# Soft mixture-of-experts on one core: 92 subtractions and additions go from VectorE to GpSimd, and two more pairs of products are split

## The chip, the cores and the metric

One Trainium2 chip, one of its cores. The metric is the device time of one execution in microseconds (us); the figure of a kernel is the median of its runs.

## The reference

Every token is multiplied with the weights of all eight experts, and the results are added with the softmax of the router's logits as weights. There are 16 x 512 = 8192 tokens of 512 features, 8 experts, and 2048 output columns:

```python
probs = softmax(router_logits)                 # 8192 x 8
output = np.zeros((batch, seq, expert_hidden))
for e in range(n_experts):
    output += probs[:, :, e:e+1] * np.matmul(x, expert_weights[e])
```

Seen as one matrix product, the left operand has 8192 rows and 8 x 512 = 4096 inner elements (x scaled by each expert's probability), the right one 4096 x 2048.

## The kernel before

**The products.** The matrix product is done with Winograd's form of Strassen's algorithm: split in two along rows, inner dimension and columns, it takes seven products of halves instead of eight, at the price of additions. The kernel does this twice. On the outer level the rows are 16 groups `q` of 512 tokens, each a block `2q` and a block `2q+1` of 256; the inner halves are experts 0 to 3 and 4 to 7; the column halves are 1024 wide. The seven outer products of a group are called P1 to P7 (`r` in the code); each has 256 tokens, 2048 inner elements and 1024 columns. On the inner level each of them is again seven *steps* (`STEPS`: 1, 5, 6, 2, 7, 3, 4). A step is eight matmuls of 128 rows, 128 inner elements and 512 columns, in float16, summed in one PSUM bank of float32. The tiles of a result are named by `tn`, the half of the tokens and the half of the columns.

**Stages.** The products are done outer product by outer product, in *stages* that mostly hold two of them (a pair), interleaved step by step: P1, then P2, then P5 and P6 mixed (a stage holds P6 of group q and P5 of group q+1; the first P6 stage and the last one hold a single product, P6 of group 0 and of group 15), then P7 and P4 in turn for the same pair of groups, then P3. A pair's stage has 14 *slots*, one for each step of each product. `k5`, `k6`, `k7` and `k3` are the numbers of the first P5 stage, the last P6 stage, the first P7 stage and the first P3 stage.

**Who does what.** TensorE does the matmuls. VectorE (`tt`, L113) makes the left operands (x times probability, minus what was there), the differences of weights, and the additions that combine a result with a base. ScalarE copies PSUM banks. GpSimd (`pool`, L127) issues stores, casts on loading and accumulating stores; it computes nothing but one mask at the start. SyncE issues the remaining loads. Each engine works through its instructions in the program's order.

**What sets the order.** The order is written out when the program is built. `at(stage, slot, f)` hangs a function on a slot. VectorE's work that is not bound to a bank is put into a queue with `later(cost, make)`: `slack` keeps one clock for TensorE and one for VectorE and takes tasks out of the queue while VectorE's clock, advanced by each task's cost, lies behind TensorE's; `need(task)` empties the queue as far as a task that is wanted now. What is not queued is issued where its function is called.

**P6's bases.** The four result tiles of P6 in group q are added on to a *base*: a kept tile of P1 (`kept`, fetched by SyncE into a tile `h`) minus P5's tile of the same name. `joined(q, tn)` (L1171) queues this subtraction with cost 0.69 in front of VectorE's queue, at slots 12, 13 and 13 of the stage before and at slot 3 of P6's own stage, for the tiles (0,0), (1,1), (0,1) and (1,0); where the stage before holds one product alone, at its slots 5, 6 and 6. `post_on_base` (L743) reads the bases when steps 1, 5, 6 and 4 are done. After step 1 it writes the sum into a new bank, and step 6 goes on in the bank that it has just read.

**The split of step 1 in P7.** In some P7 stages (`by_ones`, L1044) step 1 of the pair's two products is done as a third level: with the two products as the row halves, four inner chunks each and column halves of 256, it is seven small products of four matmuls of 256 columns. `Ones` (L622) makes what they need of the left operands: the four tiles `s[5]`, `s[6]`, `s[3]`, `s[7]` of 128 x 512 float16, one operation each (the second reads the first, the third the second), queued right behind the first halves of the two left operands, during the P4 stage before. `ones_sum` makes the four sums of the weights once, at slots 9 and 10 of the stages `ONES - 4` and `ONES - 2`; they stay until P7 and P4 are done. `ONES = k7 + 6` is the first such stage, and every second stage after it is one up to `k3`: five of the eight P7 stages.

Of the kernel before, what the change touches and what calls it, by code (L numbers as in the profile page):

```python
# [31 lines left out]
def kernel(  # L32
# [7 lines left out]
    nc = tc.nc  # L40
# [3 lines left out]
    ADD, SUB, MUL = mybir.AluOpType.add, mybir.AluOpType.subtract, mybir.AluOpType.mult  # L44
# [29 lines left out]
    def x_tile():  # L74
        return xpool.tile([P, C, HQ], f16, name="xs", tag="x")
# [7 lines left out]
    def half():  # L83
        return h_tile([P, NB], f32)
# [16 lines left out]
    def note(i):  # L101
        last[i.ins.engine] = i.ins
        if ordered[0]:
            tc.keep_in_program_order(i)

    def dve(i):
        last[i.ins.engine] = i.ins
        tc.keep_in_program_order(i)
# [3 lines left out]
    def tt(o, a, b, op):  # L112
        dve(nc.vector.tensor_tensor(out=o, in0=a, in1=b, op=op))  # L113
# [12 lines left out]
    def pool(o, i, **how):  # L126
        note(nc.gpsimd.dma_start(out=o, in_=i, **how))  # L127
# [203 lines left out]
    for n in range(2):  # L331
# [23 lines left out]
        for j in range(4):  # L355
            o = half()
# [22 lines left out]
    def flush(task):  # L379
        while task is not None and not task.done:  # L380
            queue.popleft().run()

    def need(task):
        if task is not None and not task.done:
            flush(task)
            clock["pe"] = max(clock["pe"], clock["dve"])

    def later(cost, make, first=False):
        t = Task(cost, make)
        (queue.appendleft if first else queue.append)(t)  # L390
        return t
# [70 lines left out]
    class Left:  # L462
# [11 lines left out]
        def make(self, k):  # L474
            if self.of is not None:
                need(self.of.task[k])
            if self.onto is not None:
                t = self.t[k] = self.onto.half(k)
                u = new_u()
                times(u, k, self.xb, self.pb)  # L480
                tt(t, u, t, SUB)
                return
            t = self.t[k] = new_z()
            times(t, k, self.xb, self.pb)
            if self.less is not None:
                u = new_u()
                times(u, k, *self.less)
                tt(t, t, u, SUB)
            if self.of is not None:
                tt(t, self.of.t[k], t, SUB)  # L490
            if self.kept is not None:
                tt(t, t, self.kept.half(k), SUB)
# [91 lines left out]
    class Thirds:  # L584
# [17 lines left out]
        def queue(self, whole_first=False):  # L602
            self.a.queue_make(0)
            self.b.queue_make(0)
            if whole_first:
                self.a.queue_make(1)
                self.b.queue_make(1)
            for p in (5, 6, 3, 7):
                self.task[p] = later(0.69, lambda p=p: self.make(p))
            for left in (self.a, self.b):  # L610
                left.queue_s2()
            if not whole_first:
                self.a.queue_make(1)
                self.b.queue_make(1)
# [7 lines left out]
    class Ones:  # L622
# [5 lines left out]
        def make(self, p):  # L628
            e0, e1, rows = ds(0, C), ds(C, C), ds(0, HP)
            a, b = self.a.t[0], self.b.t[0]  # L630
            if p in (5, 3):
                self.place = x_tile().rearrange("p (two c) t -> p two (c t)", two=2)
            x, y, op = {5: (b[:, e0, rows], b[:, e1, rows], ADD), 6: (5, a[:, e0, rows], SUB),
                        3: (a[:, e1, rows], 6, SUB), 7: (a[:, e0, rows], b[:, e0, rows], SUB)}[p]
            self.room[p] = self.place[:, 0 if p in (5, 3) else 1]
            o = self.room[p].rearrange("p (c t) -> p c t", c=C)
            tt(o, *(self.s[v] if isinstance(v, int) else v for v in (x, y)), op)
            self.s[p] = o

        def queue(self):  # L640
            for p in (5, 6, 3, 7):
                self.task[p] = later(0.42, lambda p=p: self.make(p))

        def op(self, r):
            need(self.task[7])
# [121 lines left out]
    def out_rows(q, odd, cols, tn):  # L767
        t, n = tn
        return out_f[ds((2 * q + odd) * HQ + t * HP, HP), ds(cols * NH + n * NB, NB)]

    def to_out(q, odd, cols, **how):
        return lambda tn, o: pool(out_rows(q, odd, cols, tn), o, **how)
# [20 lines left out]
    def at(stage, slot, make):  # L793
        hooks.setdefault((stage, slot), []).append(make)
# [6 lines left out]
    right = {r: Right() for r in (2, 5, 6, 7, 4, 3)}  # L801
    right[1] = Right(w, {p: Task(2.29, sums[p]) for p in (6, 7, 4)})
    lefts, xs, ps_, bases = {}, {}, {}, {}
# [6 lines left out]
    def left_of(r, q, fresh=True):  # L810
        a, b = 2 * q, 2 * q + 1
        if r == 1:
            pt = PBlock(a, P1, xp1[q - 2][1] if q in (2, 3) else None)
            if q in (2, 3):
                xs[a] = XBlock(a, xp1[q - 2][0])
            return Left(xblock(a), pt), [xblock(a), pt]
        if r == 2:
            pt = PBlock(a, P2)
            return Left(xblock(a), pt), [xblock(a), pt]
        if r == 7:  # L820
            pt = PBlock(b, P2)
            if q >= KEPT_Z:
                return Left(xblock(b), pt, kept=lefts[6, q]), [xblock(b), pt]
            return Left(xblock(b), pt, onto=ZHalves(q)), [xblock(b), pt]
        if r == 4:
            return Left(lefts[7, q].xb, lefts[7, q].pb), []
        if r == 5:
            pt = PBlock(b, PQ)
            return Left(xblock(b), pt), [xblock(b), pt]
        if r == 6:  # L830
            pt = PBlock(a, P1)
            return Left(xblock(a), pt, of=lefts[5, q]), [xblock(a), pt]
        if r == 3 and (q, 0) in EARLY:
            sources = {k: operand3[q, k] for k in range(2) if (q, k) in EARLY}
            if len(sources) == 2:
                return LoadedLeft(None, None, None, sources), []
            pa = PBlock(a, P2)
            return LoadedLeft(xblock(a), pa, ZHalf(q, z_places[q]), sources), [xblock(a), pa]
        if r == 3 and q < KEPT_Z:
            pt, kept_z = PBlock(a, P2), ZBlock(q)  # L840
            return Left(xblock(a), pt, kept=kept_z), [xblock(a), pt, kept_z]
        pa, pb = PBlock(a, PQ), PBlock(b, PQ)
        return Left(xblock(a), pa, (xblock(b), pb)), [xblock(a), pa, xblock(b), pb]

    def kept_rows(q):
        return lambda tn: kept[q][tn[1], ds(tn[0] * HP, HP), :]

    def product(r, q, **how):
        left, loads = left_of(r, q)
        lefts[r, q] = left  # L850
        p = None
        if r == 1:
            def sink(tn, o):
                pool(kept_rows(q)(tn), o)
            p = Product(right[1], left, sink)
        elif r == 2:
            if q >= ON_BASE or q in WITH_KEPT:
                bases[2, q] = Base(kept_rows(q))
            p = Product(right[2], left, to_out(q, 0, 0), bases.get((2, q)))
        elif r == 5:  # L860
            bases[6, q] = m1 = Base(kept_rows(q))
            m1.task = {}

            p = Product(right[5], left, to_out(q, 1, 0))
        elif r == 6:
            m1 = bases[6, q]

            def base(tn):
                need(m1.task[tn])
                return m1.t[tn]  # L870
            p = Product(right[6], left, to_out(q, 0, 1), base)
        elif r == 7:
            base = products[6, q].o.__getitem__
            if q < KEPT_Z:
                base = bases[7, q] = Base(lambda tn: out_rows(q, 0, 1, tn))
            p = Product(right[7], left, to_out(q, 1, 1), base)
        elif r == 4:
            p = Product(right[4], left, to_out(q, 1, 0, accum_op=ADD), products[7, q].o.__getitem__)
        else:
            p = Product(right[3], left, to_out(q, 0, 1, accum_op=ADD), **how)  # L880
        p.loads = loads
        products[r, q] = p
        return p

    products = {}
# [268 lines left out]
    k7 = k6 + 1  # L1154
# [14 lines left out]
    at(k6 - 1, 7, lambda: claim(products[5, 15].o, (1, 0)))  # L1169

    def joined(q, tn):  # L1171
        m1 = bases[6, q]
        m1.task[tn] = later(0.69, lambda: tt(m1.t[tn], m1.t[tn], products[5, q].o[tn], SUB), True)

    for q in range(16):
        k = k5 + 1 + q
# [270 lines left out]
    for stage, slot, q, k in ((k3 - 1, 2, 11, 0), (k3 - 1, 5, 11, 1), (k3 - 1, 7, 8, 0), (k3 - 1, 9, 5, 0),  # L1447
                              (k3 - 1, 10, 8, 1), (k3 - 1, 12, 5, 1)):
        left = lefts[3, q]
# [73 lines left out]
    def ones_sum(r):  # L1523
# [7 lines left out]
            x, y = {5: (7, 1), 6: (3, 5), 4: (2, 6), 7: (3, 7)}[r]  # L1531
            tt(ones7[r], ones7[x], ones7[y], SUB)
        later(0.69, make)
    ONES = k7 + 6
    for r, where in zip((5, 6, 4, 7), ((ONES - 4, 9), (ONES - 4, 10), (ONES - 2, 9), (ONES - 2, 10))):
        at(*where, lambda r=r: ones_sum(r))
    for stage in range(ONES, k3, 2):
        ones_[stage] = Ones(*(p.left for p in stages[stage]), ones7)
# [102 lines left out]
```

## Time and profile before

| | |
|---|---|
| median of 3 runs | 1351.62 us (1351.12 to 1351.67) |
| the profiled execution | 1351.78 us, of which its span of instructions is 1350.1 us |
| granted TensorE clock | 1.00 |
| instructions | 19508 |
| VectorE, operations and waits | 1483 operations, 1166.9 us busy |
| DMA | 346.26 MB, mean 256 GB/s |

The span is what the profiler saw from the first to the last instruction of the program; 1.7 us of the execution lie outside it. A row of a group of instructions gives line, engine, operation, output<-inputs by the program's tile names, shapes, count, then busy us and mean ns, then the idle time of the engine ahead of them. L136 is the matmul's helper, L113 VectorE's, L127 GpSimd's DMAs; since helpers have one line for everything, groups are told apart by tiles: `h<-h` is a base of P6, `xs<-z` and its kin are the quarters for the split, `ps` and `pt` are PSUM banks, `z` left operands, `d` their differences of token halves.

### The profile page before, as it was taken

The page shows a single profiled execution, that of the slowest core. Times are in us where ns is not written, and L with a number is a line of the kernel's source. Part 1 is how long each engine was busy: PE and PEld are TensorE (multiplying, and loading weights), DVE is VectorE, ACT ScalarE, POOL GpSimd, SP SyncE. Part 2 cuts the span into 40 slices and gives each one's busy share as a digit, 9 for nine tenths or more (in the row PEclk, how much of TensorE's full clock was granted, in tenths as well). Part 3 has the DMA queues.
Part 4 walks back from the last instruction along what each step waited for, and adds up shares of the span by engine and source line. Part 5 has one row for each costly group of instructions (what it writes and reads, how often), then busy time and mean ns, then how long its engine had stood idle before and what let it go on. Part 6 is the DMA issues. An engine that isn't in the chain of part 4 may idle for free.

```text
span 1350.1 us, 19508 instructions
## 1 busy us (share of the span) xinstructions
PE 1344.0 (100%) x7122; PEld 694.3 (51%) x7122; DVE 1166.9 (86%) x1483; ACT 281.9 (21%) x593; POOL 403.9 (30%) x619
## 2 busy tenths in 40 slices
PE   9999999999999999999999999999999999999998
PEld 4465655565544444444444444554555455556564
DVE  7878898989989889797897889889898989898984
ACT  3342423223211111111111100110111111224331
POOL 3123322333323232323312112424334231232342
PEclk9999999999999999999999999999999999999999
DMA  9999989989899999999998889999999989999997
GB/s 181 242 222 240 239 264 242 291 284 290 247 329 282 323 288 286 295 306 265 318 325 265 295 313 189 243 239 216 244 249 226 219 219 310 308 178 230 262 163 132
DMA packets 185392, 346.26 MB, mean 256 GB/s; under 512 B 52176, under 2 KB 81616, under 8 KB 181200
## 3 DMA queue, kind: packets, MB, share of 16 engines
q0 software_dynamic: 84960, 176.72, 58.0%
q1 hardware_dynamic: 97024, 146.15, 35.4%
q10 hardware_dynamic: 3312, 22.15, 4.6%
q8 instruction: 55, 0.90, 0.3%
q14 instruction: 41, 0.34, 0.1%
HBM read 203.19 MB, written 174.26 MB: 280 GB/s over the span
## 4 chain that ended last, share of the span: by engine, by line
PE 98%; DMA 1%; POOL 0%; issue 0%; ACT 0%; POOLq 0%
PE ps L136 77%; PE pt L136 21%; DMA w<-in_expert_weights_dram 1%; POOL w L127 0%; ACT h L1578 0%; POOL ident L234 0%; POOLq L234 0%; POOLq L1625 0%
## 5 line engine op out<-in xcount | busy, mean ns | idle before, releaser
L136 PE MATMUL ps<-w,z 128*128 128x512 f16 (+1 forms) x3884 | 840.0, 372 | 0.0
L136 PEld LDWEIGHTS <-z 128*128 128x128 f16 x5236 | 512.3, 98 | 538.1 <-issue 1.1
L127 POOL DMA_DIRECT2D out_dram<-h x380 | 251.8, 679 | 723.9 <-ACT h L751 321.9
L113 DVE TENSOR_TENSOR h<-ps,h 128x512 f32<-128x512 f32 x318 | 214.9, 686 | 59.1 <-PE ps L136 58.0
L136 PE MATMUL pt<-w,z 128*128 128x512 f16 (+1 forms) x1304 | 253.2, 338 | 0.7 <-DMA w<-in_expert_weights_dram 0.7
L113 DVE TENSOR_TENSOR z<-xT,pT 128x2048 f16<-128x2048 f16 x188 | 226.8, 1217 | 2.2 <-DMA xT<-xs 2.2
L136 PE MATMUL ps<-w,d 128*128 128x512 f16 x880 | 200.7, 379 | 0.0
L738 ACT COPY h<-ps 128x512 f32<-128x512 f32 x102 | 59.8, 586 | 394.0 <-PE ps L136 394.0
L136 PEld LDWEIGHTS <-d 128*128 128x128 f16 x880 | 86.1, 98 | 96.3
L113 DVE TENSOR_TENSOR z<-z,d 128x2048 f16<-128x2048 f16 x110 | 131.8, 1217 | 0.0
L113 DVE TENSOR_TENSOR w<-w 128x1024 f16<-128x1024 f16 (+2 forms) x106 | 116.1, 1114 | 2.6 <-PE ps L136 1.0
L113 DVE TENSOR_TENSOR d<-z 128x1024 f16<-128x1024 f16 x110 | 74.1, 685 | 1.0
L113 DVE TENSOR_TENSOR h<-pt,h 128x512 f32<-128x512 f32 x75 | 51.3, 687 | 27.0 <-PE pt L136 23.9
L751 ACT COPY h<-ps 128x512 f32<-128x512 f32 x54 | 31.6, 586 | 203.5 <-PE ps L136 203.5
L113 DVE TENSOR_TENSOR ps<-ps,h 128x256 f32<-128x256 f32 (+1 forms) x84 | 50.6, 603 | 21.0 <-PE ps L136 15.1
L734 ACT COPY h<-ps 128x512 f32<-128x512 f32 x89 | 49.9, 599 | 70.1 <-PE ps L136 61.3
L127 POOL DMA_DIRECT2D kept<-h x56 | 30.6, 547 | 86.2 <-DVE h L113 48.7
L113 DVE TENSOR_TENSOR z<-z 128x2048 f16<-128x2048 f16 (+1 forms) x52 | 50.5, 978 | 1.5
L730 ACT COPY ps<-ps 128x512 f32<-128x512 f32 x47 | 26.8, 570 | 107.4 <-PE ps L136 59.5
L113 DVE TENSOR_TENSOR h<-h 128x512 f32<-128x512 f32 (+2 forms) x69 | 45.0, 675 | 0.1
L127 POOL DMA_DIRECT2D out_dram<-kept x40 | 42.0, 1150 | 0.2 <-issue 0.2
L136 PEld LDWEIGHTS <-h 128*128 128x128 f16 x384 | 37.6, 98 | 4.3
(109 smaller groups left out, 691.7 us busy)
## 6 DMA issues: line engine op xcount, KB each, us to landing
out_dram<-h POOLq DMA_DIRECT2D x380, 256.0 KB, 7.5
z<-z SPq DMA_DIRECT2D x56, 512.0 KB, 8.7
pT<-p_dram SPq DMA_DIRECT2D x93, 256.0 KB, 8.1
h<-kept SPq DMA_DIRECT2D x88, 256.0 KB, 7.2
w<-wd ACTq DMA_DIRECT2D x20, 1024.0 KB, 8.6
w<-in_expert_weights_dram POOLq DMA_DIRECT2D x33, 512.0 KB, 12.2
xT<-x SPq DMA_DIRECT2D x63, 256.0 KB, 7.8
h<-out_dram SPq DMA_DIRECT2D x60, 256.0 KB, 8.9
```

The lines of the kernel that those rows point to most:

```text
L113: dve(nc.vector.tensor_tensor(out=o, in0=a, in1=b, op=op))
L127: note(nc.gpsimd.dma_start(out=o, in_=i, **how))
L136: note(nc.tensor.matmul(ps, z, w, start=start, stop=stop, skip_group_check=True))
L730: act(nc.scalar.copy(self.banks["b"], x))
L734: act(nc.scalar.copy(o[tn], q if p == 5 else x))
L738: act(nc.scalar.copy(o[TN[p]], b if p == 2 else x))
L751: act(nc.scalar.copy(o[tn], b))
```

## The change

`joined` no longer queues the subtraction for VectorE: it has GpSimd do it (`nc.gpsimd.tensor_tensor`) at the place where it is called, so that it stands in GpSimd's order among the stores. With the task gone, P6 takes its bases without asking for one. `Ones.make` has GpSimd do its four operations, and enters them in the queue with cost 0, so that VectorE's clock does not advance for them. `ONES` becomes `k7 + 2`: the stages `k7 + 2` and `k7 + 4` are split too, seven of the eight, and the sums of the weights are made four stages earlier, the first two of them in the stage before the last P6 stage.

```diff
@@ class Ones, make and queue
-            tt(o, *(self.s[v] if isinstance(v, int) else v for v in (x, y)), op)
+            x, y = (self.s[v] if isinstance(v, int) else v for v in (x, y))
+            note(nc.gpsimd.tensor_tensor(out=o, in0=x, in1=y, op=op))
             self.s[p] = o
...
             for p in (5, 6, 3, 7):
-                self.task[p] = later(0.42, lambda p=p: self.make(p))
+                self.task[p] = later(0.0, lambda p=p: self.make(p))
@@ product
         elif r == 5:
-            bases[6, q] = m1 = Base(kept_rows(q))
-            m1.task = {}
-
+            bases[6, q] = Base(kept_rows(q))
             p = Product(right[5], left, to_out(q, 1, 0))
         elif r == 6:
-            m1 = bases[6, q]
-
-            def base(tn):
-                need(m1.task[tn])
-                return m1.t[tn]
-            p = Product(right[6], left, to_out(q, 0, 1), base)
+            p = Product(right[6], left, to_out(q, 0, 1), bases[6, q])
@@ joined
     def joined(q, tn):
-        m1 = bases[6, q]
-        m1.task[tn] = later(0.69, lambda: tt(m1.t[tn], m1.t[tn], products[5, q].o[tn], SUB), True)
+        o = bases[6, q].t[tn]
+        note(nc.gpsimd.tensor_tensor(out=o, in0=o, in1=products[5, q].o[tn], op=SUB))
@@ the split of P7
-    ONES = k7 + 6
+    ONES = k7 + 2
```

In the built program VectorE has 80 operations fewer, GpSimd 92 more, ScalarE eight copies more, and TensorE 32 matmuls of 512 columns fewer and 56 of 256 more. Between the stores of each P6 turn GpSimd's order is now: six stores, the subtraction for (0,0), one store, those for (1,1) and (0,1), one store, and later that for (1,0). VectorE's remaining operations are the same ones, in a somewhat different order.

## The prediction

> **What bounds the kernel now.** I read the busy shares, the granted clock and the chain that ended last on the page, then TensorE's waits, then its timeline. The page first:
>
> ```profile
> PE 1344.0 (100%) x7122; PEld 694.3 (51%) x7122; DVE 1166.9 (86%) x1483; ACT 281.9 (21%) x593; POOL 403.9 (30%) x619
> PEclk9999999999999999999999999999999999999999
> PE 98%; DMA 1%; POOL 0%; issue 0%; ACT 0%; POOLq 0%
> ```
>
> TensorE is busy for 1344.0 of the 1350.1 us span, at the full granted clock, and the chain is TensorE for 98%. A busy matmul row alone does not prove that there are no holes, so the view of TensorE's waits comes next; these are all its rows (who waited, for whom, us in total, times, longest):
>
> ```profile
> PE every L95 <- DVE h L92: 1.3, 1, 1.3
> PE pt L136 <- DMA w<-in_expert_weights_dram: 0.7, 2, 0.4
> PE ps L136 <- DVE lg L304: 0.3, 1, 0.3
> ```
>
> 2.3 us of waits in all, on the warm-up, the first weights and the first logits; none is in a part that the change touches. There is thus nothing of a stall to win: the change can gain only the matmul time that it takes out, and it loses whatever stall it makes. What a matmul costs is read from its start to the next start, here in TensorE's timeline where a split P7 stage begins (start, us, ..., count):
>
> ```profile
> 922.45 0.60 PE L136 MATMUL pt<-w,z 128*128 128x256 f16 x4
> 922.89 0.60 PE L136 MATMUL pt<-xs 128*128 128x256 f16 x4
> 923.32 1.89 PE L136 MATMUL ps<-w,z 128*128 128x512 f16 x8
> 925.05 0.60 PE L136 MATMUL pt<-xs 128*128 128x256 f16 x4
> ```
>
> Four matmuls of 256 columns take 922.89 - 922.45 = 0.44 us (0.109 each when both rows are taken: 0.87 for eight), eight of 512 columns 925.05 - 923.32 = 1.73 us (0.216 each).
>
> **The change, part by part.**
>
> *Two more split pairs.* Step 1 of both products of a pair is 16 matmuls of 512 columns, 2 x 1.73 = 3.46 us. Split, it is seven small products of four matmuls of 256 columns, 28 x 0.109 = 3.05 us. That is 0.40 us less for a pair, 0.81 us for the two. TensorE has no other change of work.
>
> *What leaves VectorE.* From the groups of VectorE's instructions, shapes kept apart (count | busy us, mean ns | idle before):
>
> ```profile
> L113 DVE TENSOR_TENSOR z<-xT,pT 128x2048 f16<-128x2048 f16 x188 | 226.8, 1217 | 2.2 <-DMA xT<-xs 2.2
> L113 DVE TENSOR_TENSOR h<-h 128x512 f32<-128x512 f32 x66 | 44.0, 689 | 0.1
> L113 DVE TENSOR_TENSOR xs<-z 128x512 f16<-128x512 f16 x10 | 4.2, 422 | 0.2
> L113 DVE TENSOR_TENSOR ps<-pt,xs 128x256 f32<-128x256 f32 x10 | 4.3, 428 | 1.5 <-PE pt L136 1.5
> ```
>
> 64 of the 66 in the second row are P6's bases (4 for each of 16 products): 64 x 0.689 = 44.1 us, or 2.76 us in each P6 stage. The quarters of the five split pairs are 20 of 0.42 (the third row has ten of them): 8.4 us, 1.7 us before each. The two new pairs add four additions like the last row, 4 x 0.43 = 1.7 us, and eight small ScalarE copies. On the path this sum is zero: VectorE is not what TensorE waits for. It only widens VectorE's room.
>
> *What GpSimd gets.* 64 subtractions of 512 float32 and 7 x 4 = 28 operations on 512 float16, among the stores that it issues, in the program's order. The trace has one single computing row of GpSimd:
>
> ```profile
> L234 POOL TENSOR_SCALAR_AFFINE_SELECT ident<-ident x1: 334/334/334, 2.7 to 2.7; 128x128 f16<-128x128 f16 x1
> ```
>
> 128 elements with one input in 0.334 us. From below, the price of one subtraction is VectorE's 0.69; the row times four, with nothing taken as fixed, is 1.34; and twice that, were the second input read after the first, is 2.67. I take 1.34, the same engine's row. The Trainium skill, GPSIMD Engine Reference, section 3.1, gives 4497 ns for an addition of 2048 float32, a quarter of which would be about 1.12 us, an estimate; by it the sum would be the same. No run so far shows it.
>
> *Does it reach TensorE in P6's pair stages?* Here is the turn of two such stages, VectorE, GpSimd and TensorE from the timeline:
>
> ```profile
> 474.76 0.68 DVE L113 TENSOR_TENSOR h<-h 128x512 f32<-128x512 f32 x1
> 478.76 0.70 DVE L113 TENSOR_TENSOR ps<-ps,h 128x512 f32<-128x512 f32 x1 [0.37 <-PE ps L136]
> 482.89 0.68 DVE L113 TENSOR_TENSOR h<-pt,h 128x512 f32<-128x512 f32 x1
> ...
> 475.35 0.54 POOL L127 DMA_DIRECT2D out_dram<-h  x1 [0.26 <-issue]
> 477.24 0.54 POOL L127 DMA_DIRECT2D out_dram<-h  x1 [1.35 <-DVE h L113]
> ...
> 483.74 3.62 PE L136 MATMUL ps<-w,d 128*128 128x512 f16 x16
> ```
>
> In the changed program, base (0,0) stands behind the store of 475.35, bases (1,1) and (0,1) behind that of 477.24. So (0,0) is made from 475.89 to 477.23, and its reader, the addition at 478.76, is in time (at 2.67: 478.56, still in time). That addition itself ends 4.3 us before step 6 at 483.74 needs the bank. (1,1) and (0,1) are made by 479.12 and 480.46, the first read at 482.89. The one store queued behind them leaves after 480.46. Cost: none; the cover is 1.5 us of GpSimd's lead plus 4.3 us of VectorE's.
>
> *And in the two stages of one product*, the first of P6 and the last? There the steps of the product follow twice as fast. The first two rows are of the first such stage, the others of the last:
>
> ```profile
> 416.38 1.64 POOL L127 DMA_DIRECT2D out_dram<-h  x3 [2.45 <-DVE h L113]
> 418.32 0.70 DVE L113 TENSOR_TENSOR ps<-ps,h 128x512 f32<-128x512 f32 x1 [0.44 <-PE ps L136]
> ...
> 768.84 0.70 DVE L113 TENSOR_TENSOR ps<-ps,h 128x512 f32<-128x512 f32 x1 [0.76 <-PE ps L136]
> 770.58 0.69 DVE L113 TENSOR_TENSOR h<-pt,h 128x512 f32<-128x512 f32 x1
> 772.31 0.69 DVE L113 TENSOR_TENSOR h<-ps,h 128x512 f32<-128x512 f32 x1
> ...
> 765.97 1.14 POOL L127 DMA_DIRECT2D out_dram<-h  x2 [1.19 <-DVE h L113]
> ...
> 770.36 1.89 PE L136 MATMUL ps<-w,d 128*128 128x512 f16 x8
> ```
>
> In the last one GpSimd now does: store to 766.51, (0,0) to 767.85, store to 768.39, (1,1) to 769.73, (0,1) to 771.07. The readers are at 768.84, 770.58 and 772.31, so each is met with about 1 us to spare. If each of the three waits for one VectorE operation of 1.22 us (the mean of the kernel's commonest one), (0,1) comes at 774.7, 2.4 us late, of which VectorE's lead (the 0.8 us between 769.54 and 770.36, and the base subtraction that no longer stands behind it) takes half. From nothing to 1.2 us, then, for each of the two stages; I take 0.25 each, nearer the rows as they stand: 0.5 us.
>
> *The quarters before a split stage* are made as soon as the second left operand is ready, which the first of these rows marks:
>
> ```profile
> 913.39 0.43 DVE L113 TENSOR_TENSOR xs<-z 128x512 f16<-128x512 f16 x1
> ...
> 913.17 0.96 POOL L127 DMA_DIRECT2D out_dram<-h  x1
> ```
>
> They now begin on GpSimd behind the store, at 914.1; the first is there at 915.5, the fourth at 919.5. TensorE reads the first at 922.89 (its row stands above) and the next at 925.05: 7.4 and 5.5 us to spare. The stores queued behind them wait up to 5.4 us; base fetches wait for such stores, but are issued a stage ahead. Cost: none. The earlier places of the split (its weight sums move four stages up, beside the end of P6) put 4 x 0.69 = 2.8 us on VectorE, where 2.76 a stage have just left it: none.
>
> **The sum.** 1351.78 (the profiled execution) - 0.81 + 0.5 = 1351.47. The median of the runs is 0.16 below the profiled execution: 1351.3 us.
>
> **The rivals.** For the first, VectorE's load by stage (engine busy us and counts in windows; the fullest P6 stage, 15 of them together, the P7 and P4 part, the last single-product stage):
>
> ```profile
> 667.60:691.80 24.20, 24.20 (x113) 10.94 (x112) 23.08 (x29) 3.50 (x6) 6.97 (x13) 1.00 1.04 336
> 426.00:788.40 362.40, 362.40 (x1681) 164.31 (x1679) 308.92 (x376) 49.59 (x85) 99.24 (x175) 1.00 0.99 299
> 774.00:1151.60 377.60, 377.60 (x2014) 196.95 (x2013) 341.45 (x453) 47.06 (x109) 116.14 (x158) 1.00 0.98 243
> 764.20:776.30 12.10, 12.10 (x58) 5.49 (x57) 11.31 (x15) 1.17 (x2) 2.70 (x5) 1.00 0.73 231
> ```
>
> *1. VectorE stands still while GpSimd subtracts (slower, from a certain length on).* Should an operation of GpSimd keep VectorE from its own operations on two operands in SBUF for all of its length p, a P6 stage costs VectorE 308.92/15 = 20.6 - 2.76 + 4p of 24.16 us. It overflows when p is above (24.16 - 17.84)/4 = 1.58 us. At 1.34 it is 23.2: still hidden on the mean, and in the fullest stage (23.08) 1.5 us over, inside VectorE's lead of 4 us; the two single-product stages pay their 1.2 us each, and the time is 1351.62 - 0.81 + 2.4 = 1353.2, still within the bound. At 2.0 it is 1.7 us a stage, 15 x 1.7 = 25 us: 1376. At 2.67 it is 4.4 us a stage: 66 us, 1417. For it: the last row shows only 0.8 us of idle VectorE in the last single stage. Against it: operations with one operand in PSUM (ps and pt in the rows above) stand between VectorE's others, and the one row of GpSimd points below 1.58. The Trainium skill, SBUF — State Buffer, section "Who interferes with whom", says just this: a VectorE instruction with two SBUF inputs and a GpSimd instruction that reads SBUF exclude each other for the whole instruction. By that rule this rival is what happens, and only p decides its size; the trace of before cannot show it. Chances: 0.12 for the small form (within the bound), 0.16 for p above 1.58.
>
> *2. No exclusion, but p near 2.67.* Then the chain in the single-product stages is late by itself: in the last one (0,1) would be ready at 775.1 against 772.3, about 1.5 us of stall after VectorE's lead; in the first one (0,0) follows the first of the three stores, at 416.92, is ready at 419.6 for an addition that now starts at 418.32, and (0,1) comes at 425.5, 3.7 us late: about 2.2. The time is 1351.62 - 0.81 + 3.7 = 1354.5, just over the bound. The pair stages stay hidden, as shown. Chance 0.08.
>
> *3. Stores that come late.* Were a tile that waits for GpSimd's store missing for a base fetch, each split pair could lose a microsecond or more: 7 x 1 = 7, 1358. Against: GpSimd is busy 116.14 of 377.60 us there. Chance 0.04.
>
> *4. The split does not come about, or gains more.* The built program has 24 matmuls more (-32 of 512 columns, +56 of 256), so it comes about; with no stall to remove, 0.81 us is the most. Chance 0.02 for anything faster by 0.2%.
>
> **How the numbers follow.** The bound of 0.2%, about what a measurement of this kernel can tell from no change, is 2.7 us. The forecast (everything hidden but 0 to 1.2 us in two stages, 1350.8 to 1353.2) has 0.58; with rival 1's small form, "same" is 0.70. "Slower" is 0.16 + 0.08 + 0.04 = 0.28, "faster" 0.02. The range goes from 1350.5 (no stall at all, 0.3 for the spread of runs) up through rival 2 and most of rival 3 to 1357.0; rival 1's large form is left out.
>
> **What would show it.** Right: 56 more matmuls of 256 columns and TensorE's list of waits still near 2.3 us, without rows at L136 in P6 and P7; GpSimd rows of 1.2 to 1.4 us; VectorE's operations near them of unchanged mean length. Rival 1: VectorE's z<-xT,pT and z<-z rows longer than 1.22 where GpSimd computes, and TensorE waiting for VectorE. Rival 2: GpSimd rows of 2 us and more, with waits at the first and last P6 stage alone. The forecast is wrong if TensorE waits anywhere between 430 and 760.

## The result, and the profile after

| | median us | runs | ratio to before, 95% interval |
|---|---|---|---|
| before | 1351.61 | 1351.12 to 1351.67 | |
| after | 1370.33 | 1370.09 to 1370.63 | 1.0139 (1.0122 to 1.0157) |

The change costs 18.7 us. The forecast was 1351.3, no difference, with a range from 1350.5 to 1357.0.

The page of the kernel after, three rows of it (busy shares, granted clock by slices, engines on the chain that ended last):

```profile
PE 1348.3 (98%) x7146; PEld 697.4 (51%) x7146; DVE 1193.8 (87%) x1403; ACT 285.1 (21%) x601; POOL 537.4 (39%) x711
PEclk9999999999999999999999999999999999999999
PE 42%; DVE 0%; issue 0%; ACT 0%; DVEq 0%
```

TensorE is no longer busy for all of the span (1368.9 us). VectorE has 80 operations fewer, 51 us of work by the prediction's rows (64 x 0.689 + 20 x 0.42 - 4 x 0.43), and yet is busy 27 us longer: its remaining rows have grown. TensorE's waits in the kernel after (who for whom, us in total, times, longest):

```profile
PE ps L136 <- DVE h L113: 7.1, 7, 2.2
PE ps L136 <- DVE ps L113: 6.6, 4, 4.1
PE every L95 <- DVE h L92: 1.3, 1, 1.3
PE pt L136 <- DVE ps L113: 0.4, 1, 0.4
```

The first, second and fourth row are twelve waits for VectorE, 14.1 us, where before had none after its first microseconds. Windows of the kernel after say in which part (length, then busy us and count of TensorE, weight loads, VectorE, ScalarE, GpSimd, then granted clock, DMA share, GB/s). The first runs from where before's P6 window began to 11 us past the end of P6, the second over the rest of P7 and P4:

```profile
426.00:807.00 381.00, 369.51 (x1690) 166.09 (x1690) 333.51 (x320) 49.64 (x85) 188.29 (x235) 0.99 0.93 285
807.00:1170.00 363.00, 362.63 (x1972) 192.77 (x1971) 331.01 (x420) 49.43 (x116) 152.33 (x182) 1.00 0.95 239
```

In P6 TensorE lacks 11.5 us of 381.0 (a wait of 2.4 us lies just ahead of the window); in P7 and P4 it lacks 0.4. The loss is P6's. Taken from one matmul's start to the next, the twelve gaps are 16.0 us; two of them are followed by matmuls at half speed (below), 2.9 us more. Smaller gaps add 0.4 us: 19.3; less the 0.8 us of matmul time saved it is 18.5, against 18.8 us between the two spans. Nine of the twelve gaps, 8.9 us, lie in P6's pair stages, one each (2.4 and 4.2 us) in the two single-product stages, and one of 0.5 us in P7.

What has grown shows in the groups with shapes kept apart. First two rows of before, then the kernel after (count | busy us, mean ns):

```profile
L113 DVE TENSOR_TENSOR h<-ps,h 128x512 f32<-128x512 f32 x318 | 214.9, 686 | 59.1 <-PE ps L136 58.0 <-issue 0.9
L113 DVE TENSOR_TENSOR z<-z,d 128x2048 f16<-128x2048 f16 x110 | 131.8, 1217 | 0.0
```

```profile
L1167 POOL TENSOR_TENSOR h<-h 128x512 f32<-128x512 f32 x64 | 95.8, 1509 | 0.7
L638 POOL TENSOR_TENSOR xs<-z 128x512 f16<-128x512 f16 x14 | 19.6, 1403 | 6.2 <-DVE z L113 6.2
L113 DVE TENSOR_TENSOR z<-z,d 128x2048 f16<-128x2048 f16 x110 | 164.3, 1519 | 0.0
L113 DVE TENSOR_TENSOR h<-ps,h 128x512 f32<-128x512 f32 x326 | 218.8, 684 | 60.9 <-PE ps L136 56.6 <-issue 2.7 <-DMA out_dram<-h 1.4
```

VectorE's operations on two SBUF operands are longer; those with one operand in PSUM are not (686 and 684 ns). A mean hides how. This is a pair stage in the timeline of the kernel after: GpSimd, VectorE, TensorE (start, us):

```profile
481.06 1.28 POOL L1167 TENSOR_TENSOR h<-h 128x512 f32<-128x512 f32 x1
482.27 0.56 POOL L127 DMA_DIRECT2D out_dram<-h  x1
482.85 2.50 POOL L1167 TENSOR_TENSOR h<-h 128x512 f32<-128x512 f32 x2
485.28 0.56 POOL L127 DMA_DIRECT2D out_dram<-h  x1
...
481.35 7.74 DVE L113 TENSOR_TENSOR z<-z,d 128x2048 f16<-128x2048 f16 x2
489.01 0.69 DVE L113 TENSOR_TENSOR ps<-ps,h 128x512 f32<-128x512 f32 x1
...
489.75 2.53 PE L136 MATMUL ps<-w,d 128*128 128x512 f16 x11 [0.49 <-DVE ps L113]
```

GpSimd subtracts from 481.06, issues a store, and subtracts twice more, to 485.35. VectorE's `z<-z,d`, issued at 481.35, does not get its turn when the first subtraction ends at 482.34 nor during the store: the first of the two, taken singly, takes 5.53 us instead of 1.22 and ends 1.5 us behind the *last* of the three. The addition that TensorE waits for stands behind it. The same in the last P6 stage, where the cost is largest:

```profile
779.16 1.28 POOL L1167 TENSOR_TENSOR h<-h 128x512 f32<-128x512 f32 x1
780.37 0.56 POOL L127 DMA_DIRECT2D out_dram<-h  x1
780.95 2.50 POOL L1167 TENSOR_TENSOR h<-h 128x512 f32<-128x512 f32 x2
...
779.22 7.88 DVE L113 TENSOR_TENSOR w<-w 128x2048 f16<-128x2048 f16 x2
787.02 0.68 DVE L113 TENSOR_TENSOR ps<-ps,h 128x512 f32<-128x512 f32 x1
...
787.76 3.34 PE L136 MATMUL ps<-w,d 128*128 128x512 f16 x8 [4.07 <-DVE ps L113]
```

Two things come together here. The two `w<-w` take 7.88 us instead of 2.4. And they stand at all between the end of the stage before and the first addition: in before that place held the three base subtractions and neither of them, as its timeline shows:

```profile
766.19 1.89 DVE L113 TENSOR_TENSOR h<-h 128x512 f32<-128x512 f32 x3
```

The planner no longer advances VectorE's clock for the bases, so it pulls long operations forward into their place.

Not every P6 turn goes like these two. Taken one by one, VectorE's rows in the kernel after show an operation kept out for all three subtractions in four of the sixteen turns (3.8 to 5.0 us longer than the same operation in before), and for two back-to-back ones in four more (2.4 to 3.1 us). In the other eight the engines take turns: a `z<-z,d` issued at 531.14 runs as soon as the first subtraction ends, the next, issued at 532.65 during the second, runs before the third, and no delay in these turns is over 1.5 us. Of TensorE's eleven gaps in P6 ten, 15.1 us together, come in or behind the eight long turns (one of which cost nothing), and one of 0.35 us behind the other eight. So in this kernel the loss hangs on the long waits; why an operation gets in at once in one turn and not in another is open.

### The profile page after: what moved, and what is told of

The parts are those of the page before. It is cut to its first block, busy times and chain, and to the rows that moved or that the text cites. A ratio compares the mean times of both kernels' runs of the same rounds, so it can differ in the third digit from the quotient of the medians.

```text
span 1368.9 us, 19642 instructions
## 1 busy us (share of the span) xinstructions
PE 1348.3 (98%) x7146; PEld 697.4 (51%) x7146; DVE 1193.8 (87%) x1403; ACT 285.1 (21%) x601; POOL 537.4 (39%) x711
## 5 line engine op out<-in xcount | busy, mean ns | idle before, releaser
L136 PE MATMUL ps<-w,z 128*128 128x512 f16 (+1 forms) x3924 | 851.4, 372 | 7.1 <-DVE h L113 7.1
L136 PE MATMUL pt<-w,z 128*128 128x512 f16 (+1 forms) x1248 | 240.2, 336 | 1.0 <-DMA w<-in_expert_weights_dram 1.0
L113 DVE TENSOR_TENSOR z<-xT,pT 128x2048 f16<-128x2048 f16 x188 | 234.4, 1258 | 2.5 <-DMA xT<-xs 2.5
L113 DVE TENSOR_TENSOR z<-z,d 128x2048 f16<-128x2048 f16 x110 | 164.3, 1519 | 0.0
L113 DVE TENSOR_TENSOR w<-w 128x1024 f16<-128x1024 f16 (+2 forms) x106 | 127.5, 1225 | 5.0 <-DMA wd<-w 2.4
L1167 POOL TENSOR_TENSOR h<-h 128x512 f32<-128x512 f32 x64 | 95.8, 1509 | 0.7
L113 DVE TENSOR_TENSOR d<-z 128x1024 f16<-128x1024 f16 x110 | 80.6, 748 | 0.7
L113 DVE TENSOR_TENSOR h<-pt,h 128x512 f32<-128x512 f32 x67 | 45.4, 685 | 21.0 <-PE pt L136 18.9
L113 DVE TENSOR_TENSOR z<-z 128x2048 f16<-128x2048 f16 (+1 forms) x52 | 58.9, 1140 | 1.6
L127 POOL DMA_DIRECT2D wd<-w x45 | 24.5, 546 | 50.1 <-DVE w L113 48.8
```

Of the source, the lines that this page charges most:

```text
L136: note(nc.tensor.matmul(ps, z, w, start=start, stop=stop, skip_group_check=True))
L1167: note(nc.gpsimd.tensor_tensor(out=o, in0=o, in1=products[5, q].o[tn], op=SUB))
```

## The experiments

In the quoted expectations, A is that VectorE is held until GpSimd's whole run of subtractions is over; B is anything that needs the bases themselves to come late; C is VectorE's changed order; D is a cost of the P7 part of its own. In `e9` and `e11` B stands for the changed order, as is spelled out there. Each experiment's ratio is to before on the same chip, whose median was 1351.35 to 1351.58 there.

**Which part costs.** `e1` undoes P6's part alone; `e2` is P6's part alone.

```diff
e1 (from after): m1.task[tn] = later(0.69, lambda: tt(m1.t[tn], m1.t[tn], products[5, q].o[tn], SUB), True)
e2 (from after): Ones on VectorE, cost 0.42; ONES = k7 + 6
```

> The change without its P6 part: P6's bases are subtracted by VectorE as before, the quarters are made by GpSimd and seven pairs are split. Theory A (a VectorE operation with two SBUF operands that meets a run of GpSimd subtractions waits until the whole run is over, and the runs of three in P6 are what costs): P6 is as before and P7 keeps its 0.8 us of saved matmuls, 1350.8 to 1351.4 us. Theory B (P6's bases come late because GpSimd makes them one after another): the same, 1350.8 to 1351.4. Rival D (the quarters on GpSimd cost in P7 as well): 1352 to 1356, with waits of TensorE between 800 and 1130 us.

> The P6 part of the change alone: the bases on GpSimd, the quarters on VectorE, five split pairs. Theories A and B: all of the loss is here and only the 0.8 us (less the 0.5 of one small wait in P7) is missing, 1370 to 1371.5 us, TensorE's waits between 420 and 800 alone. Rival D: 1360 to 1368.

P6's part alone: 1370.22 us (ratio 1.0138, 1.0125 to 1.0152), the whole loss, with nearly the same waits. Without it 1355.66 (1.0038, 1.0022 to 1.0053): not the 1350.8 that the saved matmul time would give, and in D's range, not in that of A and B. So P6 costs 18.9, and the P7 part, which adds nothing clear of the noise on top of it, costs 4 us when P6 is undisturbed.

**Is it GpSimd's reading, with no base involved?** Before, with 64 idle GpSimd operations on a scratch tile at the change's places: subtractions in `e5`, four memsets each (475 ns) in `e6`, subtractions further apart in `e8`.

```diff
e5: + note(nc.gpsimd.tensor_tensor(out=scratch, in0=scratch, in1=scratch, op=SUB))   # [P, 448] f16, in joined
e6: + for i in range(4): note(nc.gpsimd.memset(scratch, 0.0))
e8: the line of e5 at the places of e3 (below)
```

> Before, whole and on VectorE, and beside it 64 GpSimd subtractions of 448 float16 elements on a tile of their own that nobody reads, at the places where the change has its base subtractions. Theory A: GpSimd's runs of three hold VectorE up although nothing waits for their result; VectorE still has its own 64 subtractions to do, so the loss is at least that of the change: 1367 to 1385 us. Theory B (late bases): no base depends on GpSimd, 1351.6 to 1352.5.

> As the run of idle subtractions, but each is four memsets of 448 float16 elements on GpSimd, which write and read nothing. If it is GpSimd's reading of SBUF that shuts VectorE's second operand out (theory A in its narrow form): no VectorE row of P6 is longer than before, 1351.6 to 1352.3 us. If any GpSimd work on SBUF shuts it out, or if it is only that GpSimd's stores leave later: above 1354.

> The 64 idle subtractions, hung on the slots that keep them apart (a store that waits stands between each two). Theory A: each holds VectorE up for at most about 1.3 us, and with VectorE's own 64 subtractions still there its load is 20.6 + up to 5.3 of 24.2 us a stage, so there is some loss, but much less than with the runs of three: 1352 to 1360 us. If the total of GpSimd's time decided: as with the idle subtractions in runs.

GpSimd's and VectorE's groups, of `e5` and then of `e6`:

```profile
L1175 POOL TENSOR_TENSOR scratch<-scratch 128x448 f16<-128x448 f16 x64 | 68.9, 1077 | 2.0
L115 DVE TENSOR_TENSOR z<-z,d 128x2048 f16<-128x2048 f16 x110 | 145.6, 1342 | 0.0
```

```profile
L1176 POOL MEMSET scratch<- 128x448 f16 x256 | 121.6, 475 | 11.9
L115 DVE TENSOR_TENSOR z<-z,d 128x2048 f16<-128x2048 f16 x110 | 131.8, 1217 | 0.0
```

`e5` 1356.54 (1.0039, 1.0026 to 1.0053), `e6` 1352.39 (1.0008, 0.9999 to 1.0017), `e8` 1354.95 (1.0025, 1.0016 to 1.0034). Subtractions that nobody needs lengthen VectorE's rows by 41 us in all and cost 5 us; memsets that keep GpSimd busy 1.8 times as long but read nothing lengthen none, and `e6` ends within 0.1 us of its first range. So no base has to come late, and what the subtractions do and the memsets do not is read SBUF. But A's size was missed: `e5` was to take at least 1367 us, and its longest delay of one VectorE row is 1.3 us, not 5. The idle subtractions each read what the one before wrote; as I read it, GpSimd pauses between them, and in the pause VectorE gets in. VectorE's total delay (41 us here, 62 in P6's part) thus does not set the loss by itself.

**Apart, broken, charged.** In `e3` the whole change has its subtractions at slots 9, 11 and 13, and slot 8 of the own stage; `e10` is the same with P6's part alone. In `e9` (P6's part, places unchanged) a small operation that reads the new tile follows each subtraction. In `e4` (before) and `e11` (P6's part) GpSimd subtracts, but VectorE's clock is still charged; `e4` does it through the old queue. `e13` is apart and charged.

```diff
e3, e10: places = ((k - 1, 9), (k - 1, 11), (k - 1, 13), (k, 8)) if duo else ((k - 1, 5), (k - 1, 6), (k, 1), (k, 8))   # (k, 5) if P6 is alone
e9:  + note(nc.gpsimd.tensor_tensor(out=scratch, in0=o[:, 0:16], in1=o[:, 16:32], op=SUB))
e4:  m1.task[tn] = later(0.69, make, True)      # make: the subtraction on GpSimd
e11: + clock["dve"] += 0.69                     # in joined; e13: also the places of e10
```

> The whole change, with the four base subtractions of a P6 product hung on other slots (9, 11 and 13 of the stage before and 8 of its own; in the single-product stages the like), so that a store that waits for a new result stands between each two of them. Theory A: no run is longer than one subtraction, VectorE's longest wait in P6 falls from 5.0 to about 1.3 us, inside its lead of some 4 us, and the time is 1351 to 1354. If VectorE's total loss decided (four times 1.3 to 1.5 us a stage whether together or apart), the time would stay at 1365 to 1371. Theory B would expect some gain too, as the bases are ready earlier.

> Before, with one edit: P6's bases are still queued with cost 0.69 at their old places, so that VectorE's other work keeps its order of before, but GpSimd does the subtraction. Theory C (what costs is the new order: the clock thinks that VectorE has time and puts long operations ahead of the additions that TensorE waits for): 1351 to 1354 us. Theory A: the runs of three are still there, 1363 to 1373.

> P6's part of the change alone, its subtractions at the same places and VectorE's order the same, but each subtraction is followed by a small one on GpSimd that reads the tile just written (16 columns), so that GpSimd must wait between two of them. Theory A (a VectorE operation on two SBUF operands waits until GpSimd's whole run of subtractions is over): the longest VectorE row falls from 6.2 us to about 2.7 us (one subtraction more than its own 1.2), and most of the 18.9 us goes: 1352 to 1358 us. Theory B (what counts is VectorE's changed order, whatever the runs): 1366 to 1371 us.

> P6's part alone with its subtractions apart (slots 9, 11, 13 of the stage before and 8 of the own one), five split pairs as before. Theory A with the split as a cost of its own (the split of seven pairs costs some 4 us by itself, as with everything on VectorE): 1351.3 to 1353 us. Rival (what was left in the whole change with the subtractions apart, 4 us, is still P6's): 1354.5 to 1356.5 us.

> P6's part alone, at the change's places, but VectorE's clock advances by 0.69 us at each subtraction, so that VectorE's long operations are spread as if it still made the bases. Theory A alone: the runs of three stay, 1366 to 1371 us. Theory B (the order that the uncharged clock gives): 1353 to 1358 us. Both by halves: 1358 to 1364 us.

> P6's part alone, five split pairs, its subtractions apart and VectorE's clock advanced by 0.69 us at each. If runs and VectorE's order are the whole cause: 1351.3 to 1352.5 us, with no wait of TensorE for VectorE above 0.3 us in P6. If the exclusion costs by itself, even one subtraction at a time: 1353 to 1356 us, as with the subtractions apart alone.

The last column of the table is the most by which a VectorE row in P6 is longer than rows of its group in before.

| P6's subtractions on GpSimd | median us | ratio, 95% interval | longest delay of a VectorE row in P6, us |
|---|---|---|---|
| as in the change (`e2`) | 1370.22 | 1.0138 (1.0125 to 1.0152) | 4.9 |
| charged, old queue (`e4`) | 1361.31 | 1.0074 (1.0061 to 1.0087) | 5.1 |
| charged (`e11`) | 1360.07 | 1.0060 (1.0047 to 1.0072) | 4.9 |
| runs broken (`e9`) | 1357.58 | 1.0050 (1.0037 to 1.0062) | 2.0 |
| apart (`e10`) | 1354.35 | 1.0018 (1.0009 to 1.0027) | 2.2 |
| apart and charged (`e13`) | 1353.08 | 1.0008 (0.9999 to 1.0017) | 2.5 |
| apart, whole change (`e3`) | 1355.63 | 1.0039 (1.0024 to 1.0053) | 2.1 |

VectorE with its runs broken, GpSimd beside it (timeline of `e9`, a pair stage):

```profile
480.46 1.68 DVE L114 TENSOR_TENSOR z<-xT,pT 128x2048 f16<-128x2048 f16 x1
482.17 1.23 DVE L114 TENSOR_TENSOR z<-z 128x2048 f16<-128x2048 f16 x1
...
479.38 1.68 POOL L1167 TENSOR_TENSOR h<-h 128x512 f32<-128x512 f32 x1
481.14 1.08 POOL L1168 TENSOR_TENSOR scratch<-h 128x16 f32<-128x16 f32 x1
482.18 2.34 POOL L1167 TENSOR_TENSOR h<-h 128x512 f32<-128x512 f32 x1
```

Now the engines take turns: VectorE's `z<-xT,pT` loses 0.46 us, and it is GpSimd's next subtraction that waits (2.34 instead of 1.28). That recovers 12.6 of the 18.9 us with VectorE's order as in the change. Charging the clock alone, with the runs left as they are, recovers 10.2, the "both by halves" of its forecast. They overlap; as I read it, a costly wait needs both: a run of subtractions, and long VectorE operations between it and an addition that TensorE waits for. Apart recovers 15.9, apart and charged 17.1; the intervals of these two overlap, so what charging adds there is not shown.

Not all of these forecasts held. `e3` and `e10` are 1.6 and 1.4 us above the ranges that A gave them, and `e13` lies in the range for "the exclusion costs by itself", not in that for runs and order as the whole cause. And no single number of the table sorts these kernels: VectorE's delays of more than 0.3 us in P6 sum to 38 us in `e9` and in `e13`, the longest is shorter in `e9`, and yet `e9` loses 6.1 us and `e13` 1.5. Where VectorE's operations stand beside the subtractions counts as well.

What stands ahead of the addition in the last P6 stage, in the timelines of `e3` (not charged) and `e13`:

```profile
765.53 5.17 DVE L113 TENSOR_TENSOR w<-w 128x2048 f16<-128x2048 f16 x2
770.62 0.68 DVE L113 TENSOR_TENSOR ps<-ps,h 128x512 f32<-128x512 f32 x1
```

```profile
767.79 1.45 DVE L113 TENSOR_TENSOR w<-w 128x2048 f16<-128x2048 f16 x1
770.65 0.70 DVE L113 TENSOR_TENSOR ps<-ps,h 128x512 f32<-128x512 f32 x1 [1.41 <-PE ps L136]
```

In `e3` two `w<-w` delay the addition, and TensorE loses 1.5 us there; in `e13` one does, VectorE is early and waits for TensorE. This is not charging alone, for `e3` has seven split pairs and `e13` five; `e10`, not charged and with five, loses nothing there in its profiled run. The only wait of TensorE for VectorE left in `e13`'s P6 is 1.2 us (forecast: none above 0.3) in the first, single-product stage, where VectorE's 2.5 us delay stands. `e4` falls between the ranges of C and A and tests neither cleanly, since it keeps a cost of its own: the queue is filled at its front, so of the run of three (0,0) is made last, and VectorE waits for it (VectorE's waits, then the timeline of `e4`):

```profile
DVE ps L113 <- POOL h L1174: 17.2, 4, 6.1
```

```profile
417.28 3.71 POOL L1174 TENSOR_TENSOR h<-h 128x512 f32<-128x512 f32 x3
421.02 0.70 DVE L113 TENSOR_TENSOR ps<-ps,h 128x512 f32<-128x512 f32 x1 [5.70 <-POOL h L1174]
```

**The P7 part by itself.** `e12` makes the quarters on GpSimd with five split pairs, `e14` with six; `e7` is before with seven and everything on VectorE; `e15` is `e1` with the sums of the weights behind P6.

```diff
e12: from e1, ONES = k7 + 6      e14: from e1, ONES = k7 + 4      e7: from before, ONES = k7 + 2
e15: from e1, sums at (k7, 9), (k7, 10), (k7 + 1, 9), (k7 + 1, 10)
```

> Before, with seven split pairs and nothing on GpSimd: quarters and bases by VectorE. TensorE's work is that of the change, 0.8 us less than before: 1350.8 to 1351.2 us if VectorE has room for 2 x 4 more quarters of 0.42 us and four additions in the early P7 part; above 1352 if the GpSimd part was needed for the two new pairs.

> The quarters alone are made by GpSimd, P6's bases on VectorE, five split pairs as before. If the 4 us that the change costs without P6's bases come from the two new split pairs: 1351.2 to 1352.2 us. If they come from GpSimd making the quarters (stores held up behind them, or VectorE held): 1354 to 1357 us.

> Quarters by GpSimd, P6's bases on VectorE, six split pairs: the sums of the weights begin in the first P7 stage, no longer beside the last P6 stage. If the 4 us of the seven pairs come from the sums beside P6 and from what that stage delays: 1351.0 to 1351.8 us (0.4 less matmul time than with five). If every further split stage costs: 1353 to 1355 us.

> Seven split pairs, quarters by GpSimd, P6's bases on VectorE, and the sums of the weights made in the two stages after the last P6 stage. If the sums beside P6 are the cause: 1350.8 to 1352 us and no wait near 781 us. If each further split stage costs some 0.5 us and P6's end 1.6 us: 1353 to 1354.5 us, with short waits at the four-column-block products of the split stages.

`e12` 1351.78 (1.0006, 0.9997 to 1.0015): the quarters on GpSimd cost nothing. `e14` 1354.54 (1.0022, 1.0010 to 1.0035), `e15` 1355.72 (1.0029, 1.0016 to 1.0041), `e7` 1356.97 (1.0041, 1.0028 to 1.0054): each further split pair takes 0.4 us of matmuls away, and yet six or seven pairs are 3.0 to 5.4 us slower than before. `e15` is above both of its ranges. TensorE's waits and a stretch of the timeline (VectorE, TensorE) in `e7`, then TensorE's and VectorE's waits in `e15`:

```profile
PE pt L136 <- DVE ps L113: 2.8, 8, 0.4
PE ps L136 <- DVE z L113: 1.4, 1, 1.4
```

```profile
883.07 0.42 DVE L113 TENSOR_TENSOR ps<-pt,xs 128x256 f32<-128x256 f32 x1
...
883.54 0.60 PE L136 MATMUL pt<-d,z 128*128 128x256 f16 x4 [0.37 <-DVE ps L113]
```

```profile
PE pt L136 <- DVE ps L113: 2.0, 3, 1.3
PE ps L136 <- DVE h L113: 1.6, 2, 1.1
...
DVE h L113 <- DMA out_dram<-h: 5.9, 5, 3.3
```

The split needs a bank back at its last small product, and with seven pairs VectorE's addition that frees it is about half a us late in each of the seven split stages of `e7`; the eighth wait of that row is in the P4 stage at 857 us. Once, beside the last P6 stage, TensorE waits 1.56 us (start to start) for a left operand: its `z<-z,d` stands behind a sum of the weights and starts at 774.04, 2.9 us later than in before. These waits of `e7` are 5.7 us; less the 0.8 of matmul time saved that is 4.9, all of the difference between its span (1355.0) and that of before. `e15` has no wait near 781 us, as meant, and is no faster: it waits in P7 instead, there also through VectorE, which waited 5.9 us for stores. The times of `e14` and `e15` scatter (1351.4 to 1360.3 and 1352.8 to 1357.7), and a profile shows one execution, so how their loss divides between late bank reads and late stores stays open, and so does why more pairs make VectorE's addition late.

## Why the prediction was wrong, point by point

*TensorE has no stalls, the gain is 0.8 us at most.* Right as a bound, but no kernel reached it: with seven pairs and P6 undisturbed it was 4.3 to 5.4 us slower (`e1`, `e15`, `e7`), not 0.8 faster.

*What leaves VectorE: "It only widens VectorE's room."* Wrong: with 51 us of operations gone VectorE was busy 27 us longer, because its remaining operations on two SBUF operands grew.

*The price of a subtraction, 1.34 us.* Right: 1.28 where nothing hinders it (481.06 above); the mean of 1.51 contains GpSimd's own waits.

*P6's pair stages: "Cost: none; the cover is 1.5 us of GpSimd's lead plus 4.3 us of VectorE's".* This step failed: the pair stages, priced at nothing, lost 8.9 us. It followed the bases to their readers, and in the stage shown they do come in time. It did not follow what VectorE does meanwhile. There one operation held for the run and the store in it (4.3 us from 481.06 to 485.35) uses up the lead of 4.3, and the one behind it adds the rest.

*The single-product stages, 0.25 us each.* This step failed too: the first lost 2.4 and the last 4.2 us, each with 1.5 more at half speed. Three separate waits of 1.22 us of *GpSimd* were priced; it was VectorE that was held, in one piece, for two subtractions in the first and for all three in the last. The last stage's 0.8 us of idle VectorE, quoted for rival 1, was the warning.

*Rival 1, VectorE held while GpSimd subtracts.* The mechanism is this one, and its sign in the trace (longer `z<-xT,pT` and `z<-z` rows, TensorE waiting for VectorE) came as written. Its price by mean load was wrong: at p = 1.34 it gave 23.2 us of VectorE in a 24.16 us stage, "still hidden on the mean", and 1353.2. The kernel came out at 1370.3 with p = 1.28, below the threshold of 1.58. The mean load is not what decides: `e5` and `e2` show 41 and 62 us of delay for 5 and 19 us of loss, and in the first window above VectorE was idle for 47.5 of 381 us while TensorE waited for it. As far as the runs show, what counts is whether one wait outlasts VectorE's lead over TensorE, by its length and by what stands behind it. The Trainium skill, SBUF — State Buffer, section "Who interferes with whom", which the prediction weighed, is borne out in what excludes what: rows with two SBUF operands grow, those with one in PSUM (686, 684 ns) do not, and beside memsets none does. It puts the exclusion at one instruction; so it went in eight of the sixteen P6 turns, while in four a waiting VectorE operation stayed out through two subtractions and in four through three and a store.

*"VectorE's remaining operations are the same ones, in a somewhat different order."* The order had no term in the sum. Charging the clock alone is worth 10.2 us (`e11` against `e2`).

*The quarters: none.* Right (`e12`). *The weight sums moved to P6's end: none.* Wrong where P6's bases remain on VectorE: 1.56 us in `e1` and `e7`; with them on GpSimd it cannot be told from the 4.2 us there.

*Rival 3, late stores.* Not in the kernel after. In `e15` VectorE waits for stores (5.9 us, five times), so the mechanism exists; why the kernel after shows little of it is open. *Rival 2* fell with p = 1.28.

## What to carry to other kernels

Work moved to GpSimd that reads SBUF is not beside VectorE's two-operand work but in turn with it. Ask how long the longest run of such GpSimd instructions is, since a VectorE operation can be kept out for all of it, and which operation, and whose reader, can be caught behind it; the mean load answers neither. Break such runs with a dependency or with distance, and when a planner orders the engine by a clock, go on charging it for the time the moved work still takes from it. On an engine that has no stalls, taking work off its neighbour gains nothing, so any new wait decides the result.

## What the runs showed of the hardware

- A VectorE operation on two SBUF operands that is issued while GpSimd subtracts waits for the end of that subtraction, and it can miss its turn there: in the kernel after it stayed out for two or three subtractions in eight of sixteen P6 turns, in four of them across a store issue of 0.56 us (delays up to 5.0 us for subtractions of 1.28 us), and got in after one in the other eight. What decides between the two is open. A store issue alone does not hold it: in before 508 such operations overlap with a DMA issue of GpSimd, and none takes more than 0.01 us over the median of its group. With a dependency between GpSimd's instructions the longest delay was 1.3 us in `e5` and 2.0 in `e9`.
- After some waits TensorE runs at half speed for a while: eight matmuls take 3.34 us at 787.76, where the prediction's last row of the same stage shows 1.89. Seven to nine matmuls start 427 ns apart, some 1.5 us more. The page's row of granted clock stays at 9 because one of its slices is 34 us long; over 788.03 to 791.45 and over 426.22 to 429.63, 3.41 us each, the granted clock is 0.50, and in all these traces it changes only at multiples of 3.41 us. Cut each trace, without its start and end, into these steps: every step at full clock in which TensorE was idle for 2.08 us or more (nine of them, in six runs) is followed by one at half, and none with 1.87 us or less is. So the place of a wait counts beside its length. A wait of 2.2 us in `e2` lay in one step (2.08 idle) and halved the clock; one of 2.1 us in the kernel after (0.58 and 1.32) and one of 2.8 us in `e4` (1.30 and 1.35) lay across two and did not. The Trainium skill, TensorE: Matmul & The Clock Gate, Part 1, describes a clock halved after an idle window of about 3.4 us that runs freely, with 426.7 ns for such a matmul; the length of the window and the 427 ns agree, but here about 2.1 us of idle time in one window were enough.
